# Attention scores in a hybrid layer: two of three partial products stacked into one 128-row product, the third kept as 64-row pairs

## The chip, the cores and the metric

One Trainium2 chip; the kernel runs on one of its cores. The metric is the device time of one execution in microseconds (us). An engine is named as the profile names it: PE is TensorE's matmul, PEld its weight load, DVE VectorE, ACT ScalarE, POOL GpSimd, SP the engine that issues most DMAs.

## What is computed

A decoder layer over 2048 positions with width 1024: one input projection, an attention branch of 16 heads of 64 (causal, three dilations, a window of 128 steps, linear position bias), a state-space branch, an output projection of both and a layer norm. The part that matters here, for one dilation:

```python
# q pre-scaled; blocks of 128 positions of one residue; kk, vv: previous and current block
scores = jnp.einsum('bnqrhe,bnkrhe->bnrhqk', qb, kk).astype(jnp.float32)
scores = jnp.where(valid[:, None, None], scores + bias, -jnp.inf)
lse = jax.nn.logsumexp(scores, axis=-1)
p = jnp.exp(scores - lse[..., None]).astype(vv.dtype)
o = jnp.einsum('bnrhqk,bnkrhe->bnqrhe', p, vv)
...
o1, l1 = dilated_window_attention(q, k, v, slopes, DILATIONS[0])   # 1
o2, l2 = dilated_window_attention(q, k, v, slopes, DILATIONS[1])   # 4
o3, l3 = dilated_window_attention(q, k, v, slopes, DILATIONS[2])   # 16
wts = jax.nn.softmax(jnp.stack([l1, l2, l3], axis=0), axis=0)
y_att = wts[0][..., None] * o1 + wts[1][..., None] * o2 + wts[2][..., None] * o3
```

## The kernel before

The products that need float32 precision are taken with a split of each operand into a high part, rounded to fp32r, and a low part, the remainder. A product of two split operands is a sum of three: high x high, high x low, low x high.

The first stage is the input projection (`proj`, lines 102 to 112): 128 output channels at a time against 4 x 512 positions, each 512-wide bank the sum of 8 x 3 products. `fin_qk` (lines 121 to 132) evicts q and k: ScalarE writes the high part, VectorE the low one, and each goes to its own array in device memory, `d_qh`, `d_ql`, `d_kh`, `d_kl`, one for each pair of heads. Between the projections runs the state-space branch (`ssd`, lines 322 to 393).

The second stage is attention over 8 pairs of heads. A pair of heads fills the 128 partitions: head 0 in rows 0 to 63, head 1 in rows 64 to 127. `load_pair` (lines 426 to 447) loads the bias tables and v on SP's queue, and the four parts of q and k on POOL's. The tiles of q and k lie in two pools, `qk[0]` and `qk[1]`, which pairs use in turn. `permute` (lines 460 to 474) rewrites both parts of q on POOL in the order that dilation 4 or 1 wants, into `qp` (four buffers).

A pair has 24 steps: three values of `d`, four of `qd`, two of `half`; a step covers two blocks of 128 queries. `d` = 0 is dilation 16, where a residue has just one block of 128 and so none before it; `d` = 1 is dilation 4 and `d` = 2 dilation 1, with a previous block for all but the first of each residue. `permute` serves `d` = 1 and `d` = 2.

`first` (line 476) says where there is no previous block; there the scores are 128 keys wide, else 256. `scores` (lines 479 to 521) takes, for a block, the three products for both heads, each with 64 rows of contraction, the two heads one after the other (line 503), then adds the bias and takes the row's minimum on VectorE (line 511), then the exponential on ScalarE (line 519). `transposes` (line 532) turns the weights on TensorE, VectorE copies them from PSUM to `PT` (line 534), and `values` (line 552) multiplies them with v, with both heads in 64 columns each; ScalarE copies the sums to `num` (lines 557 to 562).

The order on TensorE is written out by hand (lines 746 to 772): in turn `i` come the scores of step `i`, the transposes of step `i - 2` and the values of step `i - 3`. The order on the other engines is the planner's, by a simulated time. At the end of a pair `statistics` transposes row minima and sums, writes them to `d_st`, `gather` reads them back as `cm`, and `combine` (lines 588 to 629) works out the weights of the three dilations on VectorE, sends them through `d_wd` and, on POOL (line 613), multiplies the numerators `num` (four buffers, of which a pair takes three).

The third stage is the output projection (`product`, lines 693 to 716). Its weights are split by `load_w1` and `load_w2` into tiles that attention has done with, by the names in `ring`.

Of the kernel before, what the change touches and what calls it, by code (L numbers as in the profile page):

```python
# [9 lines left out]
F32 = mybir.dt.float32  # L10
F32R = mybir.dt.float32r
# [17 lines left out]
def hybrid_layer(ctx, tc, xT, xc, w52, wv, convw, convb, dtb, alog, dskp, gcol, wout,  # L29
# [14 lines left out]

    d_qh = [dtile(f"d_qh{i}", [128, S]) for i in range(8)]
    d_ql = [dtile(f"d_ql{i}", [128, S]) for i in range(8)]
    d_kh = [dtile(f"d_kh{i}", [128, S]) for i in range(8)]
# [26 lines left out]
    with ExitStack() as c1:  # L74
# [46 lines left out]
        def fin_qk(i, scale):  # L121
            def f(ps, tb):
                hi = ev.tile([128, 512], F32R, name="ev")
                lo = ev.tile([128, 512], F32, name="ev")
                nc.scalar.activation(hi, ps, AF.Copy, scale=scale)  # L125
                nc.vector.scalar_tensor_tensor(lo, ps, scale, hi.bitcast(F32), op0=OP.mult,  # L126
                                               op1=OP.subtract)
                s = slice(tb * 512, tb * 512 + 512)
                dh, dl = (d_kh, d_kl) if scale == 1.0 else (d_qh, d_ql)
                nc.sync.dma_start(dh[i][:, s], hi.bitcast(F32))  # L130
                nc.sync.dma_start(dl[i][:, s], lo)
            return f
# [281 lines left out]
    with ExitStack() as c2:  # L414
# [11 lines left out]
        def load_pair(pr):  # L426

            A = {"pr": pr, "num": [], "tab": [], "v": [], "cur": {}}
            for d in range(3):
                tb = io.tile([128, 2, (128, 256, 256)[d]], F32, name=f"tb{d}", bufs=1)  # L430
                c0 = (512, 256, 0)[d]
                nc.sync.dma_start(tb, tabs[2 * pr:2 * pr + 2, :, c0:c0 + tb.shape[2]]
                                  .rearrange("h p c -> p h c"))
                A["tab"].append(tb)
            A["q"], A["k"] = {0: []}, []
            for x, src in (("q", d_qh), ("k", d_kh), ("q", d_ql), ("k", d_kl)):
                to = A["q"][0] if x == "q" else A["k"]
                t = qk[pr % 2].tile([128, NR, NJ], F32R, name=f"{x}{'hl'[len(to)]}")
                nc.gpsimd.dma_start(f2(t), src[pr])
                to.append(t)  # L440
            for d in range(3):
                v = io.tile([128, 16, 128], F32, name="v", bufs=3)
                nc.sync.dma_start(v, d_v[d][:, :, pr * 128:pr * 128 + 128]
                                  .rearrange("b p e -> p b e"))
                A["v"].append(v)
            A["st"] = stp.tile([128, 192], F32, name="st")
            return A
# [30 lines left out]

        def scores(A, d, qd, half):

            P = io.tile([128, 2, 2, 256], F32, name="P", bufs=3)
            tab = A["tab"][d]
            sp = [psS.tile([128, 512], F32, name="S") for h in range(2)]
            for b in range(2):
# [11 lines left out]
                else:  # L496
                    kv = lambda t: t[:, :, 8 * blk + 8 - w // 16:8 * blk + 8].rearrange(
                        "p r (h j) -> p r h j", j=8)
                    ov = lambda a: a.rearrange("p (h r j) -> p r h j", r=16, j=8)
                for m, (x, y) in enumerate(((0, 0), (0, 1), (1, 0))):  # L500
                    for h in range(2):
                        hr = slice(64 * h, 64 * h + 64)
                        nc.tensor.matmul(ov(sp[h][:, 256 * b:256 * b + w]), A["q"][d][x][hr, blk],  # L503
                                         kv(A["k"][y][hr]), start=(m == 0), stop=(m == 2))
            for h in range(2):
# [126 lines left out]
        ring = {"qp": (io, 4), "v": (io, 3), "num": (cm_, 4), "wb": (cm_, 3)}  # L632
        ring.update({f"{x}{p}{i}": (qk[i], 1) for x in "qk" for p in "hl" for i in range(2)})
        W, SP, u7, free, os_ = {}, {}, [], [], []

        def big(name, dt=F32R):
            pool, n = ring[name]
            return f2(pool.tile([128, NR, NJ], dt, name=name if n > 1 else name[:2], bufs=n))

# [49 lines left out]

        UT = ["v", "v", "kl1"]  # L690
        banks = [("S", psS), ("S", psS), ("S", psS), ("S", psS), ("T", psT), ("T", psT)]
# [54 lines left out]
        with tc.manual_schedule(engines={mybir.EngineType.PE}):  # L746
            for i in range(len(todo) + TA + 1):
                if i < len(todo):
# [42 lines left out]
        load_u(2, 1, row())  # L791
        load_w1(2, "kh1")
        os_ += [raw, r0]
# [89 lines left out]
```

## Time and profile before

| | us |
|---|---|
| median of 3 runs | 2262.6 (2258.39 to 2266.82) |
| profiled execution, its own time | 2261.54 |
| its span, first to last instruction | 2259.7 |
| PE busy | 2176.9 (96%) |
| PEld busy | 1815.1 (80%) |
| DVE busy | 1142.9 (51%) |
| ACT busy | 871.2 (39%) |
| POOL busy | 754.1 (33%) |
| mean granted TensorE clock | 0.966 |

A line of the order of time reads: start, length, engine, line of the kernel, operation, what is written `<-` what is read, the shape of the weights (rows of contraction * columns) and of the moving operand, and how often. Lengths of matmuls overlap, since they are pipelined; what a matmul costs in a stream is the distance between starts. Starts there count from the first instruction of any kind. A line of waits reads: who waited `<-` for whom, total us, times, the longest one.

### The profile page before, as it was taken

What the parts mean: (1) busy time and instruction counts of PE and PEld (TensorE: products, weight loads), DVE (VectorE), ACT (ScalarE), POOL (GpSimd) and SP (SyncE); (2) the same over time, 40 slices, a digit from 0 to 9 for tenths busy, and PEclk for the clock granted to TensorE, in tenths of its full rate; (3) what the DMA queues carried; (4) which work ended last, traced back from release to release, by engine and by line L of the source; (5) the groups of instructions that cost most, each with busy time, mean ns of one, the idle gap of its engine ahead of it and who ended that gap; (6) DMA issues with size and microseconds to landing.
All of it is one profiled execution on the core that took longest, in us unless ns stands there. A gap on an engine that the chain in (4) does not pass through costs nothing. (4 is left out here: it accounts for less than half of the span.)

```text
span 2259.7 us, 36859 instructions
## 1 busy us (share of the span) xinstructions
PE 2176.9 (96%) x13968; PEld 1815.1 (80%) x13968; DVE 1142.9 (51%) x2931; ACT 871.2 (39%) x2318; POOL 754.1 (33%) x511
## 2 busy tenths in 40 slices
PE   8999999999999999999999998889889989899998
PEld 8999888888888888888888787677777767688886
DVE  3000365562004455545434287767767886855553
ACT  4101122213112232323454376667666774322221
POOL 3100011010113555555555214446435763222121
PEclk9999999999999999999999798889888999999999
DMA  8544222222226455555543735756674656423220
GB/s 286 167 142 125 79 68 82 75 66 80 84 71 208 163 195 179 173 178 173 179 138 108 275 108 159 202 161 180 175 205 140 169 144 207 161 99 101 79 84 28
DMA packets 232449, 321.69 MB, mean 142 GB/s; under 512 B 27088, under 2 KB 166736, under 8 KB 224080
## 3 DMA queue, kind: packets, MB, share of 16 engines
q1 hardware_dynamic: 227664, 285.78, 41.5%
q0 software_dynamic: 4608, 33.56, 4.2%
q8 instruction: 110, 1.80, 0.3%
q14 instruction: 67, 0.55, 0.1%
HBM read 205.65 MB, written 113.64 MB: 141 GB/s over the span
## 5 line engine op out<-in xcount | busy, mean ns | idle before, releaser
L109 PE MATMUL pp<-xh,whi 128*128 128x512 f32 x1408 | 550.1, 391 | 0.0
L110 PE MATMUL pp<-xl,whi 128*128 128x512 f32 x1408 | 549.5, 390 | 0.0
L111 PE MATMUL pp<-xh,wlo 128*128 128x512 f32 x1408 | 548.7, 390 | 0.0
L519 ACT ACTIVATE P<-P,st 128x256 f32<-128x256 f32 (+1 forms) x768 | 345.2, 451 | 122.2 <-DVE st L511 122.0
L511 DVE CUSTOM_DVE_ANT_0 P<-S,tb 128x256 f32<-128x256 f32 (+1 forms) x768 | 234.7, 360 | 152.9 <-PE S L503 108.7
L111 PEld LDWEIGHTS pp<-xh,wlo 128*128 128x128 f32 x1408 | 264.4, 188 | 55.0
L109 PEld LDWEIGHTS pp<-xh,whi 128*128 128x128 f32 x1408 | 264.4, 188 | 54.8
L110 PEld LDWEIGHTS pp<-xl,whi 128*128 128x128 f32 x1408 | 264.5, 188 | 54.2
L99 POOL TENSOR_TENSOR wlo<-wraw,whi 128x1024 fp32r<-128x1024 f32 x44 | 106.0, 2409 | 490.0 <-ACT whi L98 490.0
L552 PE MATMUL N<-PT,v 128*64 128x128 f32 x2400 | 192.3, 301 | 49.1 <-DVE PT L534 24.1
L552 PEld LDWEIGHTS N<-PT,v 128*64 128x64 f32 x2400 | 140.9, 148 | 86.8 <-DVE PT L534 27.3
L534 DVE COPY PT<-T 128x512 f32<-128x512 f32 (+1 forms) x304 | 196.7, 676 | 2.8 <-PE T L532 2.7
L532 PE MATMUL T<-ident,P 128*128 128x128 f32 x1200 | 189.6, 298 | 7.6 <-ACT P L519 3.7
L532 PEld LDWEIGHTS T<-ident,P 128*128 128x128 f32 x1200 | 138.2, 149 | 32.9 <-ACT P L519 5.3
L519 ACT ACTIVATION_READ_ACCUMULATOR P<-P,st 128x1 f32 x768 | 144.0, 187 | 0.0
L613 POOL TENSOR_TENSOR wb<-num,wb 128x2048 f32<-128x2048 f32 x21 | 95.3, 4550 | 144.9 <-DMA wb<-d_wd 73.4
L126 DVE SCALAR_TENSOR_TENSOR ev<-pp,ev 128x512 f32<-128x512 f32 x64 | 44.1, 688 | 195.8 <-ACT ev L125 194.8
L503 PE MATMUL S<-kh,qp 64*128 64x256 f32 (+1 forms) x1024 | 140.6, 332 | 0.0
L503 PEld LDWEIGHTS S<-kh,qp 64*128 64x128 f32 x1024 | 99.7, 212 | 25.9 <-issue 24.3
L361 DVE TENSOR_SCALAR mt<-csb,cs 128x128 f32<-128x128 f32 x256 | 72.3, 353 | 74.9 <-DMA csb<-d_cs 74.9
L152 PE MATMUL pp<-vh,xh 128*128 128x384 f32 (+1 forms) x304 | 95.0, 320 | 5.5 <-ACT xh L182 5.4
L98 ACT CAST whi<-wraw 128x1024 fp32r<-128x1024 f32 x44 | 46.0, 1046 | 137.6 <-PE pp L110 134.6
(281 smaller groups left out, 3753.1 us busy)
## 6 DMA issues: line engine op xcount, KB each, us to landing
v<-d_v SPq DMA_DIRECT2D x24, 1024.0 KB
wb<-d_wd SPq DMA_DIRECT2D x48, 512.0 KB
wraw<-w SPq DMA_DIRECT2D x44, 512.0 KB
csb<-d_cs SPq DMA_DIRECT2D x32, 512.0 KB
d_v<-vt SPq DMA_DIRECT2D x64, 192.0 KB
d_za<-ev SPq DMA_DIRECT2D x32, 256.0 KB
d_xs<-cvo SPq DMA_DIRECT2D x8, 1024.0 KB
d_zs<-ez SPq DMA_DIRECT2D x8, 1024.0 KB
```

Source lines behind the costliest of these rows:

```text
L99: nc.gpsimd.tensor_tensor(lo, raw, hi.bitcast(F32), op=OP.subtract)
L109: nc.tensor.matmul(ps, hi[:, k, :], h, start=(k == 0), stop=False)
L110: nc.tensor.matmul(ps, hi[:, k, :], l, start=False, stop=False)
L111: nc.tensor.matmul(ps, lo[:, k, :], h, start=False, stop=(k == 7))
L152: nc.tensor.matmul(ps, h, vw[k][0], start=(k == 0), stop=False)
L503: nc.tensor.matmul(ov(sp[h][:, 256 * b:256 * b + w]), A["q"][d][x][hr, blk], kv(A["k"][y][hr]), start=(m == 0), stop=(m == 2))
L511: nc.vector.tensor_tensor_reduce(P[:, h, b, 256 - w:256], sp[h][:, c0:c0 + w], tab[:, h, tab.shape[2] - w:], 1.0, 3.0e38, OP.add, OP.min, ...
L519: nc.scalar.activation(p, p, AF.Exp, bias=stat(A, 0, d, h, blk), scale=-1.0, accum_out=stat(A, 1, d, h, blk))
L532: nc.tensor.transpose(tp[:, h, b], P[:, h, b, 128 * which:128 * which + 128], ident)
L534: nc.vector.tensor_copy(pt[:, :, bl[0]:2], tp[:, :, bl[0]:2])
L552: nc.tensor.matmul(nm[64 * h:64 * h + 64, bq * 128:bq * 128 + 128], v[:, k, 64 * h:64 * h + 64], pts[which][:, h, b], start=(f or not whic ...
L613: eng.tensor_tensor(wb, nums[d], wb, op=OP.mult)
```

## The change

The q parts are stored per head and stacked: for head 0 the high part in rows 0 to 63 and the low part in rows 64 to 127, for head 1 the low part first. The high part of k is loaded twice over, so that a tile `kh[h]` holds the same 64 rows in both halves. One product of 128 rows is then high x high plus low x high. The third product, high q x low k, is taken from the same stacked tile's high half as a 64-row product, for both heads one after the other. The full products come first in a turn, then the transposes, then the 64-row ones, then the values. The stacked tiles `qs` lie in the pool `io` with two buffers, so all pairs share them; `kh0`, `kh1` and `kl` take turns as before. The names of free tiles for the output weights follow.

```diff
-    d_qh = [dtile(f"d_qh{i}", [128, S]) for i in range(8)]
-    d_ql = [dtile(f"d_ql{i}", [128, S]) for i in range(8)]
+    d_qs = [dtile(f"d_qs{i}", [2, 128, S]) for i in range(8)]
...
-                dh, dl = (d_kh, d_kl) if scale == 1.0 else (d_qh, d_ql)
-                nc.sync.dma_start(dh[i][:, s], hi.bitcast(F32))
-                nc.sync.dma_start(dl[i][:, s], lo)
+                hi = hi.bitcast(F32)
+                if scale == 1.0:
+                    nc.sync.dma_start(d_kh[i][:, s], hi)
+                    nc.sync.dma_start(d_kl[i][:, s], lo)
+                else:
+                    nc.sync.dma_start(d_qs[i][0, 0:64, s], hi[0:64])
+                    nc.sync.dma_start(d_qs[i][1, 64:128, s], hi[64:128])
+                    nc.sync.dma_start(d_qs[i].rearrange("a p t -> (a p) t")[64:192, s], lo)
...
-            A["q"], A["k"] = {0: []}, []
-            for x, src in (("q", d_qh), ("k", d_kh), ("q", d_ql), ("k", d_kl)):
-                to = A["q"][0] if x == "q" else A["k"]
-                t = qk[pr % 2].tile([128, NR, NJ], F32R, name=f"{x}{'hl'[len(to)]}")
-                nc.gpsimd.dma_start(f2(t), src[pr])
-                to.append(t)
+            A["q"] = {0: [io.tile([128, NR, NJ], F32R, name="qs", bufs=2) for h in range(2)]}
+            A["kh"] = [qk[pr % 2].tile([128, NR, NJ], F32R, name=f"kh{h}") for h in range(2)]
+            A["kl"] = qk[pr % 2].tile([128, NR, NJ], F32R, name="kl")
+            for h in range(2):
+                nc.gpsimd.dma_start(f2(A["q"][0][h]), d_qs[pr][h])
+                for i in range(2):
+                    nc.gpsimd.dma_start(f2(A["kh"][h][64 * i:64 * i + 64]), d_kh[pr][64 * h:64 * h + 64])
+            nc.gpsimd.dma_start(f2(A["kl"]), d_kl[pr])
...
-        def scores(A, d, qd, half):
-
-            P = io.tile([128, 2, 2, 256], F32, name="P", bufs=3)
-            tab = A["tab"][d]
-            sp = [psS.tile([128, 512], F32, name="S") for h in range(2)]
+        def products(A, d, qd, half, low, sp):
             for b in range(2):
...
-                for m, (x, y) in enumerate(((0, 0), (0, 1), (1, 0))):
-                    for h in range(2):
-                        hr = slice(64 * h, 64 * h + 64)
-                        nc.tensor.matmul(ov(sp[h][:, 256 * b:256 * b + w]), A["q"][d][x][hr, blk],
-                                         kv(A["k"][y][hr]), start=(m == 0), stop=(m == 2))
+                for h in range(2):
+                    hr = slice(64 * h, 64 * h + 64) if low else slice(0, 128)
+                    k = A["kl"] if low else A["kh"][h]
+                    nc.tensor.matmul(ov(sp[h][:, 256 * b:256 * b + w]), A["q"][d][h][hr, blk], kv(k[hr]),
+                                     start=not (low or b), stop=bool(low and b), skip_group_check=True)
+
+        def scores(A, d, qd, half, sp):
+            P = io.tile([128, 2, 2, 256], F32, name="P", bufs=3)
+            tab = A["tab"][d]
+            products(A, d, qd, half, True, sp)
...
-                    pts[i] = scores(pairs[pr], d, qd, half)
+                    sp = [psS.tile([128, 512], F32, name="S") for h in range(2)]
+                    products(pairs[pr], d, qd, half, False, sp)
                 if 0 <= i - TA < len(todo):
                     pr, d, qd, half = todo[i - TA]
                     pts[i - TA] = transposes(d, qd, half, pts[i - TA])
+                if i < len(todo):
+                    pr, d, qd, half = todo[i]
+                    pts[i] = scores(pairs[pr], d, qd, half, sp)
...
-        r0 = big("kl0", F32)
-        load_w2(8, r0, "qh0", "kh0")
-        load_w2(10, r0, "ql0", "num")
+        r0 = big("kl_0", F32)
+        load_w2(8, r0, "kh0_0", "kh1_0")
+        load_w2(10, r0, "qs", "num")
...
-        load_w2(14, r0, "qh1", "ql1")
+        load_w2(14, r0, "qs", "kl_1")
...
-        load_w1(2, "kh1")
+        load_w1(2, "kh0_1")
```

More of the change, by code (lines that the diff above doesn't have):

```diff
@@ L632, in hybrid_layer @@
         ring = {"qp": (io, 4), "v": (io, 3), "num": (cm_, 4), "wb": (cm_, 3)}
-        ring.update({f"{x}{p}{i}": (qk[i], 1) for x in "qk" for p in "hl" for i in range(2)})
+        ring.update({f"{x}_{i}": (qk[i], 1) for x in ("kh0", "kh1", "kl") for i in range(2)})
+        ring["qs"] = (io, 2)
         W, SP, u7, free, os_ = {}, {}, [], [], []
@@ L637, in big @@
             pool, n = ring[name]
-            return f2(pool.tile([128, NR, NJ], dt, name=name if n > 1 else name[:2], bufs=n))
+            return f2(pool.tile([128, NR, NJ], dt, name=name.split("_")[0], bufs=n))
         def prep_w(e, raw, name, eng):
@@ L688, in load_u @@
             nc.vector.reciprocal(r, r)
-        UT = ["v", "v", "kl1"]
+        UT = ["v", "v", "kh1_1"]
         banks = [("S", psS), ("S", psS), ("S", psS), ("S", psS), ("T", psT), ("T", psT)]
```

## The prediction

> **What bounds the kernel now.** I read the stretches by stage first, then the order of single instructions on TensorE, then who waited for whom. The stretches: time, busy time of PE, PEld, DVE, ACT and POOL with counts, granted clock, DMA share, GB/s.
>
> ```profile
> 0.00:1265.00 1265.00, 1258.89 (x6447) 1071.02 (x6448) 469.96 (x731) 340.20 (x497) 380.11 (x289) 1.00 0.43 139
> 1265.00:1856.00 591.00, 534.15 (x5750) 433.57 (x5748) 439.50 (x1865) 411.70 (x1632) 276.48 (x185) 0.89 0.61 171
> ```
>
> The projections hold TensorE for 1259 of 1265 us. Attention, from 1265 to 1856, is what the change is about: 591 us, TensorE busy 534, but at a granted clock of 0.89. So it loses time twice: 57 us idle, and a share of the rest at the lower clock. Next, one step of dilation 1, with 256-wide blocks, at full clock: scores S, transposes T, values V.
>
> ```profile
> 1557.71 1.09 PE L532 MATMUL T<-ident,P 128*128 128x128 f32 x8
> 1558.73 1.09 PE L552 MATMUL N<-PT,v 128*64 128x128 f32 x16
> 1559.75 0.39 PE L503 MATMUL S<-kh,qp 64*128 64x256 f32 x2
> 1559.98 0.29 PE L503 MATMUL S<-kl,qp 64*128 64x256 f32 x2
> 1560.10 0.42 PE L503 MATMUL S<-kh,qp 64*128 64x256 f32 x4
> 1560.35 0.29 PE L503 MATMUL S<-kl,qp 64*128 64x256 f32 x2
> 1560.47 0.29 PE L503 MATMUL S<-kh,qp 64*128 64x256 f32 x2
> 1560.69 1.09 PE L532 MATMUL T<-ident,P 128*128 128x128 f32 x8
> ```
>
> T 1.02, V 1.02, S 0.94 us: 2.98 a step, with no idle between. The two 64-row products of a pair (one for each head) start together, and pairs follow each other at (1560.47 - 1559.98) / 4 = 0.12 us: **twelve products take six slots**. Beside the slots a block pays at its edges: the first pair holds 0.23 instead of 0.12, and from the last pair's start to the transposes it is 0.22. A light step (dilation 16, 128-wide blocks), also at full clock:
>
> ```profile
> 1349.45 0.33 PE L503 MATMUL S<-kh,qh 64*128 64x128 f32 x2
> 1349.61 0.28 PE L503 MATMUL S<-kl,qh 64*128 64x128 f32 x2
> 1350.06 0.27 PE L503 MATMUL S<-kh,ql 64*128 64x128 f32 x2
> 1350.26 0.66 PE L532 MATMUL T<-ident,P 128*128 128x128 f32 x4
> 1350.85 0.66 PE L552 MATMUL N<-PT,v 128*64 128x128 f32 x8
> 1351.44 0.33 PE L503 MATMUL S<-kh,qh 64*128 64x128 f32 x2
> ```
>
> Here S is 0.81, T 0.59, V 0.59, the step 1.99; a pair's slot is (1350.06 - 1349.61) / 4 = 0.11, the first 0.16, the last to T 0.20. The waits (total, times, longest) say where the idle time comes from:
>
> ```profile
> PE N L552 <- DVE PT L534: 24.1, 8, 6.8
> DVE mm L592 <- DMA cm<-d_st: 22.0, 7, 7.4
> PE N L552 <- ACT num L559: 20.8, 6, 4.4
> ACT num L559 <- POOL wb L613: 16.2, 7, 5.0
> ```
>
> Once a head pair VectorE stands in `combine` for the statistics to land, and values wait for the copy behind it; and once the copy of numerators waits for the buffer that the previous pair's combination frees. The change touches neither chain.
>
> **The change part by part.**
>
> *Two products as one, 128 rows deep.* Of six slots for each block, four (two pairs) become two full products, and one pair stays: 2 + 1 = 3 slots for each 128-query block, as before. So everything hangs on what a full 128-row product of 256 columns costs. The trace has none, but the value projection has 128x128 weights against 272 columns; these are the first and last of 27 in a row, and then a product of 512 columns followed by transposes, and one followed by a 64-column shape:
>
> ```profile
> 204.72 0.29 PE L152 MATMUL pp<-vh,xh 128*128 128x272 f32 x1
> 208.00 0.29 PE L154 MATMUL pp<-vh,xl 128*128 128x272 f32 x1
> ...
> 693.71 0.39 PE L110 MATMUL pp<-xl,whi 128*128 128x512 f32 x1
> 693.94 0.39 PE L111 MATMUL pp<-xh,wlo 128*128 128x512 f32 x1
> 694.17 0.60 PE L337 MATMUL ss<-ident,xs 128*128 128x128 f32 x4
> ...
> 701.77 0.39 PE L109 MATMUL pp<-xh,whi 128*128 128x512 f32 x1
> 702.09 0.33 PE L368 MATMUL ss<-mt,xdt 128*64 128x128 f32 x2
> ```
>
> 3.28 / 26 = 0.126 us for 272 columns and 0.23 for 512; on that line 256 columns take 0.12, the very slot of a pair. For 128 columns, the four transposes at 694.17 follow at (0.60 - 0.27) / 3 = 0.11, again a pair's slot (0.27 is the length of a lone one, as in the pairs' rows). Bounds for 256 columns: 0.11 and 0.126. I take 0.12: the work in slots does not fall.
>
> [...]
>
> *The order H, T, L, V* (H the full products, L the 64-row pairs). The rows above show what an edge costs: from 512 columns to transposes with the same 128*128 shape it is 0.23 us, no more than between two products (693.71 to 693.94 is also 0.23); to the 128*64 shape it is 0.32, so 0.09 for the change of shape, and then a longer first interval. H to T keeps the shape and is free. Before there were three changes of shape (V-S, S-T, T-V), after there are three (V-H, T-L, L-V). Heavy step: H = 0.23 + 3 x 0.12 = 0.59; T loses its long first interval: three intervals there are (0.66 - 0.27) = 0.39 in the light step and 0.33 at 694.17, so 1.02 - 0.06 = 0.96; L = 0.23 + 0.22 = 0.45; together 2.00 against S + T = 1.96: +0.04. Light step: H 0.16 + 3 x 0.11 = 0.49, T 0.53, L 0.16 + 0.20 = 0.36: 1.38 against 1.40: -0.02. A head pair has 14 steps with a 256-wide block and 10 without; 8 x 14 x 0.04 - 8 x 10 x 0.02 = **+3 us**. Bounds: with the slot at 0.11, 112 x 4 x 0.01 = 4.5 less, so -1.5; at 0.126, 2.7 more, so +6.
>
> *Scores are complete later.* L ends behind T, and the next-but-one T starts earlier in its step. The path in the light step:
>
> ```profile
> 1351.33 0.69 DVE L534 COPY PT<-T 128x512 f32<-128x512 f32 x1
> 1352.27 0.19 ACT L519 ACTIVATION_READ_ACCUMULATOR P<-P,st 128x1 f32 x1
> 1352.37 0.56 ACT L557 COPY num<-N 128x512 f32<-128x512 f32 x1
> ```
>
> From the last pair (1350.06) the exponentials are done at 1352.46; their transposes start at 1350.26 + 2 x 1.99 = 1354.24: 1.8 us to spare. After, the last pair starts at 0.49 + 0.53 + 0.16 = 1.18 of its step (0.61 before) and T at 0.49 (0.81 before): 0.9 are left. The copy PT of 0.69, which now becomes ready ahead of the scores, takes about 0.3 of it, and the copy of the numerators (0.56, every second step) can take the rest. So light steps may wait by tenths. Heavy steps had more time and keep about a microsecond. Bounds: 0, and 0.1 in each of 64 light steps, +6. I take **+2**, because a light stage that runs longer shortens the wait for numerators (20.8 us above), which is counted from the end of the pair before. PT, in turn, gains the length of L before V needs it, 0.3 us in each of the eight waits, too little to count.
>
> *Loads.* Per head pair POOL issues seven DMAs for four and moves 5 MB for 4.
>
> ```profile
> 1239.61 0.75 POOL L439 DMA_DIRECT2D qh<-d_qh  x1 [0.31 <-POOL y L383]
> 1240.88 0.55 POOL L439 DMA_DIRECT2D ql<-d_ql  x1
> 1245.84 2.29 POOL L467 CAST qp<-qh 128x512 fp32r<-128x512 f32 x4 [3.40 <-DMA qh<-d_qh]
> 1251.47 2.29 POOL L467 CAST qp<-ql 128x512 fp32r<-128x512 f32 x4 [3.35 <-DMA ql<-d_ql]
> ```
>
> ```profile
> POOL qh L439 <- PE S L503: 54.1, 4, 15.4
> ```
>
> Three issues of 0.55 are 1.6 us on POOL, a queue that stood idle for 54 us in front of just these loads. `qs` has two buffers, so a pair's loads wait for the light stage before it and for the second permutation; they land some 10 us later (1240.88, the issue of `ql`, to 1251.47), and the first user, a permutation, comes with the first steps of dilation 1. Zero, with that as its cover. For head pair 0 `qs` lies in the pool that takes over the projections' memory and could come late: the most is the landing again, +11; I take 0, since the first half of the activations is done 22 us (96 products of 0.23) before the end. [...] The output weights prepared in `qs` and `kl_1` find them free once the last scores are done, about where the first product starts: 0 to +2, taken +1.
>
> Sum: 3 + 2 + 1 = **+6 us**. Against the profiled execution's 2261.5 that is 2267.5; the median of the runs lies 1.1 above it, so I say **2268**, 0.2% slower than the median. What this measurement can tell from no change is about 0.5%, 11 us.
>
> **Rivals.**
>
> *The light stages slip to the lower clock (slower).* The pace of light stages differs, by window of TensorE (length, busy, granted clock, DMA):
>
> ```profile
> 1265.40:1291.30 25.90, 21.01 (x161) 0.61 0.96 309
> 1339.10:1359.10 20.00, 18.34 (x227) 1.00 0.62 190
> 1485.90:1515.00 29.10, 22.28 (x249) 0.86 0.43 127
> ```
>
> Eight light steps took 25.9 us at 0.61 and 20.0 at 1.00. The stage at 1485.90 shows that idle time and a lower clock go together: 6.8 us idle, 0.86. If the thin slack makes TensorE pause in light stages, half the pairs going from the second to the first pace cost 4 x 5.9 = 24: 2292 with the sum. It decides once pauses recur in most light stages. [...] 0.22.
>
> *H and T count as different modes.* Then a fourth edge, 0.09 plus 0.06, in 192 steps: +29, 2296. Against it stand 693.94 to 694.17. [...] 0.05.
>
> *The DVE order moves (faster).* If the copies PT, now ready first, let `combine` meet its statistics later, the 22.0 us in which VectorE stood for `cm` go: 2245. For: they are one instruction's place in a queue. Against: program order keeps four steps between the two. 0.12.
>
> *Four products for six is a gain of a third.* If each product cost half a pair's slot, 4 x 0.06 in 112 steps and 4 x 0.055 in 80 go: -45, 2218. The 0.126 of the 272-column row speaks against it. 0.04.
>
> *No change of the above kind:* 0.57 for the forecast, with 2252 to 2276 as its own range.
>
> **The numbers.** Slower by over 0.5% (above 2274): the first two rivals and a tail of the forecast, 0.30. Faster (below 2251): the other two and a little, 0.17. Same 0.53. The range takes in the prices of the first and the third rival: 2245 to 2292.
>
> **What would show it.** Right: full products at 0.12 (0.11 for 128 columns) apart, H to T without an edge, a heavy step of about 3.0 us, light 1.98. Wrong: idle TensorE in front of T with ScalarE as releaser, a clock in 1265 to 1856 other than 0.89 by some hundredths, `cm` waits that differ by over 10 us in total, or the first scores starting well after the last projection. The wait for numerators is what I expect to give a little.

## The result and the profile after

The changed kernel takes 2340.95 us (median of 4 runs, 2337.57 to 2341.43) against 2263.48 for the kernel before (4 runs, 2258.39 to 2266.82): a ratio of 1.0341, interval 1.0319 to 1.0363. It is slower by 77 us; the profiled execution has a span of 2339.6 and a mean granted clock of 0.951.

Attention as a whole, from its first scores to its last values, in the kernel before and in the kernel after (length, busy time of PE, PEld, DVE, ACT, POOL with counts, granted clock, DMA share, GB/s):

```profile
1265.40:1879.10 613.70, 556.20 (x5951) 451.62 (x5950) 454.39 (x1901) 422.84 (x1664) 290.75 (x189) 0.89 0.61 173
```

```profile
1267.20:1955.30 688.10, 570.62 (x5178) 466.58 (x5177) 450.74 (x1901) 422.52 (x1664) 299.26 (x214) 0.85 0.61 165
```

The projections, up to 1265, are as they were, with TensorE busy for 1258 us. Attention is 74 us longer. TensorE is busy 571 us of it where it was 556, at a granted clock of 0.85 where it was 0.89, and idle 117 us where it was 58: most of the loss is idle time, and a slower clock goes with it. The steps themselves are hardly longer. TensorE in order of time, a light step, then a heavy step (256-wide blocks) and what follows, both steps at full clock:

```profile
1436.63 0.64 PE L509 MATMUL S<-kh,qs 128*128 128x128 f32 x4
...
1438.62 0.67 PE L509 MATMUL S<-kh,qs 128*128 128x128 f32 x4
...
1560.98 0.74 PE L509 MATMUL S<-kh,qp 128*128 128x256 f32 x4
1561.56 1.03 PE L544 MATMUL T<-ident,P 128*128 128x128 f32 x8
1562.53 0.51 PE L509 MATMUL S<-kl,qp 64*128 64x256 f32 x4
1562.96 1.09 PE L564 MATMUL N<-PT,v 128*64 128x128 f32 x16
1563.99 0.74 PE L509 MATMUL S<-kh,qp 128*128 128x256 f32 x4
...
1571.69 0.69 PE L564 MATMUL N<-PT,v 128*64 128x128 f32 x4 [5.66 <-ACT num L571]
```

From 1560.98 to 1563.99 the heavy step takes 3.01 us (2.98 before), the light one 1.99 (1.99 before). The last line shows where time is lost: values that stand for 5.66 us on the copy of numerators. The waits of the kernel after (total, times, longest):

```profile
DVE mm L604 <- DMA cm<-d_st: 58.7, 6, 14.5
PE N L564 <- ACT num L571: 51.9, 7, 9.7
PE N L564 <- DVE PT L546: 51.7, 6, 12.9
ACT num L571 <- POOL wb L625: 29.2, 7, 6.2
```

These are the four rows that the prediction showed of before, and each has grown: 22.0 to 58.7, 20.8 to 51.9, 24.1 to 51.7, 16.2 to 29.2. They are two links of one chain. VectorE stands for the gathered statistics `cm`, so the copy `PT` behind it is late and the values wait; and because the combination ends late, the buffer of numerators comes free late. That chain belongs to `statistics`, `gather` and `combine`, of which the change edits no line.

**What reaches that chain, for more than half of the loss, is the loads.** First their rate. The table by windows for the kernel before, in a stretch with only k loads on the way (128 partitions each), and one with the weights `wb` (64 partitions each, for which one row is read 64 times):

```profile
1344.00:1348.00 4.00, 4.00 (x59) 3.30 (x55) 2.64 (x11) 2.79 (x15) 0.00 (x0) 1.00 1.07 428
1530.00:1540.00 10.00, 7.46 (x90) 6.14 (x86) 8.75 (x32) 7.20 (x28) 4.03 (x1) 1.00 1.04 221
```

and for the kernel after, the `kh` loads into 64 partitions and the `qs` loads into 128:

```profile
1428.00:1434.00 6.00, 6.00 (x72) 5.13 (x68) 4.96 (x23) 4.28 (x18) 5.98 (x11) 1.00 1.16 233
1620.00:1622.00 2.00, 0.00 (x0) 0.00 (x0) 0.00 (x0) 0.00 (x0) 2.00 (x1) 0.88 1.07 422
```

The last two columns say it: all transfer engines fully busy in each, but 428 and 422 GB/s into 128 partitions, 221 and 233 into 64. The changed kernel loads `kh` as four halves, 2 of its 5 MB a pair, and the page's row for POOL's queue (packets, MB, share of the engines' time) of the kernel before and after:

```profile
q0 software_dynamic: 4608, 33.56, 4.2%
```

```profile
q0 software_dynamic: 6016, 41.95, 6.3%
```

25% more bytes take 4.2% of 2259.7 = 95 us of all transfer engines before and 6.3% of 2339.6 = 147 after, 55% more. The rows show the rates; what makes the half they do not show.

Second, who waits. One pair's end in the kernel after, several engines in order of time (start, length; SP lines are issues of transfers):

```profile
1509.75 2.13 POOL L447 DMA_DIRECT2D kh<-d_kh  x4
...
1520.23 0.26 ACT L584 COPY sT<-N 64x128 f32<-64x128 f32 x1
1520.52 10.26 SPq L592 DMA_DIRECT2D d_st<-sT  x4
1529.03 1.08 POOL L445 DMA_DIRECT2D qs<-d_qs  x2 [12.14 <-PE S L509]
1538.01 0.30 SPq L598 DMA_DIRECT2D cm<-d_st  x1
1540.02 0.28 DVE L604 TENSOR_TENSOR mm<-cm 32x128 f32<-32x128 f32 x1 [14.32 <-DMA cm<-d_st]
1553.82 0.54 DVE L613 TENSOR_TENSOR cm<-cm,mm 32x384 f32<-32x384 f32 x1
1566.52 4.50 POOL L625 TENSOR_TENSOR wb<-num,wb 128x2048 f32<-128x2048 f32 x1 [36.41 <-DMA wb<-d_wd]
1571.05 1.07 ACT L571 COPY num<-N 128x512 f32<-128x512 f32 x2 [2.11 <-POOL wb L625]
```

and the same places in the kernel before:

```profile
1494.78 0.59 POOL L439 DMA_DIRECT2D kh<-d_kh  x1
...
1496.94 0.26 ACT L572 COPY sT<-N 64x128 f32<-64x128 f32 x1
1497.22 7.98 SPq L580 DMA_DIRECT2D d_st<-sT  x4
1507.53 0.30 SPq L586 DMA_DIRECT2D cm<-d_st  x1
1509.53 0.28 DVE L592 TENSOR_TENSOR mm<-cm 32x128 f32<-32x128 f32 x1 [7.38 <-DMA cm<-d_st]
...
1513.38 0.59 POOL L439 DMA_DIRECT2D qh<-d_qh  x1 [12.88 <-PE S L503]
...
1535.97 4.52 POOL L613 TENSOR_TENSOR wb<-num,wb 128x2048 f32<-128x2048 f32 x1 [21.47 <-DMA wb<-d_wd]
```

In both kernels the k loads go out just ahead of the statistics. From the first store of the statistics to the load of `cm` (which waits for the stores to land, 19.4 us in all eight pairs of before) it is 10.3 us before and 17.5 after. The q loads are let go by the scores of the light stage; before, they went out at 1513.38, after `cm` had landed; after, the k loads are slower, and the q loads come at 1529.03, while the statistics are still under way. By the table by windows, in steps of 3 us, the share of the transfer engines is 1.06 or more from 1512 to 1536 in the kernel after, and the stores have landed at 1538; in the kernel before it falls to 0.14 at 1506.

A quantity that I use below: **the way**, from the end of ScalarE's copy of the second statistics to the end of POOL's first multiplication, when the next pair's numerators get their buffer. In the lines above it is 1520.49 to 1571.02 = 50.5 after, 1497.20 to 1540.49 = 43.3 before. It has three parts: landing (to the first minimum, `mm`), combination (to the end of its last product), and the rest (weights out through `d_wd`, back, first multiplication). The mean over seven pairs, worked out for each kernel from the records of these four instructions in its profiled execution:

| | landing | combination | rest | way | first statistics |
|---|---|---|---|---|---|
| before | 8.8 | 8.8 | 20.1 | 37.6 | 1348.2 |
| after | 14.8 | 14.5 | 17.7 | 47.0 | 1357.8 |

The last column is when the first pair's statistics are copied, so 9.6 us is the later start. 9.6 + 7 x 9.4 = 75 of the 77 us. The way had grown by 6.0 in the landing and 5.7 in the combination, and lost 2.4 in the rest.

### The profile page after: what moved, and what is told of

Same layout as the page of the kernel before. It is cut to its first block, busy times and chain, and to the rows that moved or that the text cites. A ratio compares the mean times of both kernels' runs of the same rounds, so it can differ in the third digit from the quotient of the medians.

```text
span 2339.6 us, 35693 instructions
## 1 busy us (share of the span) xinstructions
PE 2195.3 (94%) x13200; PEld 1834.4 (78%) x13200; DVE 1144.1 (49%) x2931; ACT 871.4 (37%) x2318; POOL 767.9 (33%) x535
## 3 DMA queue, kind: packets, MB, share of 16 engines
q0 software_dynamic: 6016, 41.95, 6.3%
## 4 chain that ended last, share of the span: by engine, by line
PE 81%; DMA 6%; issue 6%; POOL 3%; DVE 2%; SPq 1%; ACT 1%; DVEq 0%; POOLq 0%; ACTq 0%
PE pp L110 13%; PE pp L108 13%; PE pp L109 13%; PE S L509 6%; PE N L564 5%; PE T L544 4%; PE S L724 3%; PE S L726 3%; PE S L725 3%; PE pp L158 2%; PE pp L156 2%; PE pp L157 2%; DMA wb<-d_wd 2%; PE T L724 1%; PE T L725 1%
## 5 line engine op out<-in xcount | busy, mean ns | idle before, releaser
L564 PE MATMUL N<-PT,v 128*64 128x128 f32 x2400 | 195.4, 305 | 104.8 <-ACT num L571 51.9
L523 DVE CUSTOM_DVE_ANT_0 P<-S,tb 128x256 f32<-128x256 f32 (+1 forms) x768 | 233.6, 358 | 39.0 <-DMA tb<-tabs 37.6
L544 PE MATMUL T<-ident,P 128*128 128x128 f32 x1200 | 184.9, 295 | 3.8 <-DVE PT L546 2.7
L544 PEld LDWEIGHTS T<-ident,P 128*128 128x128 f32 x1200 | 147.4, 152 | 5.5 <-ACT P L531 3.2
L509 PE MATMUL S<-kh,qp 128*128 128x256 f32 (+1 forms) x512 | 107.9, 340 | 0.0
L509 PEld LDWEIGHTS S<-kh,qp 128*128 128x128 f32 x512 | 80.8, 221 | 25.7 <-issue 22.4
```

The costliest lines, as they stand in the source:

```text
L523: nc.vector.tensor_tensor_reduce(P[:, h, b, 256 - w:256], sp[h][:, c0:c0 + w], tab[:, h, tab.shape[2] - w:], 1.0, 3.0e38, OP.add, OP.min, ...
L544: nc.tensor.transpose(tp[:, h, b], P[:, h, b, 128 * which:128 * which + 128], ident)
L564: nc.tensor.matmul(nm[64 * h:64 * h + 64, bq * 128:bq * 128 + 128], v[:, k, 64 * h:64 * h + 64], pts[which][:, h, b], start=(f or not whic ...
```

## The experiments

**Is it the order of scores and transposes?** Put the order back in the changed kernel (e3), and split it in the kernel before (e4).

```diff
 # e3, from the changed kernel
                     products(pairs[pr], d, qd, half, False, sp)
+                    pts[i] = scores(pairs[pr], d, qd, half, sp)
                 if 0 <= i - TA < len(todo):
...
-                if i < len(todo):
-                    pr, d, qd, half = todo[i]
-                    pts[i] = scores(pairs[pr], d, qd, half, sp)
```

```diff
 # e4, from the kernel before: two of three pairs of products, transposes, the third pair
-                for m, (x, y) in enumerate(((0, 0), (0, 1), (1, 0))):
+                for x, y in ((0, 1),) if low else ((0, 0), (1, 0)):
...
-                    pts[i] = scores(pairs[pr], d, qd, half)
+                    sp = [psS.tile([128, 512], F32, name="S") for h in range(2)]
+                    products(pairs[pr], d, qd, half, False, sp)
...
+                if i < len(todo):
+                    pr, d, qd, half = todo[i]
+                    pts[i] = scores(pairs[pr], d, qd, half, sp)
```

> The changed kernel with the 64-row products put directly behind the full ones, ahead of the transposes, as all scores were before; loads as changed. One more change of array shape is not made: H-L, L-T, T-V, V-H are four against three. Theory O: the time falls to 2265 to 2285. Theories H and B: it stays between 2330 and 2370, the upper end from the fourth edge (0.09 to 0.15 us in 192 steps).

Measured: 2342.82 us, ratio 1.0347 (1.0323 to 1.0371), as the changed kernel. Its steps are longer by the fourth change of shape (heavy 3.14 us against 3.01, light 2.14 against 1.99, some 27 us of TensorE's time in all), so taken alone this run could hide a gain from the old order.

> The kernel before with the order of the change alone: two of the three products (as 64-row pairs still) ahead of the transposes, the third behind them; loads and tiles as before. It has two more changes of array shape in a turn (V-S, S-T, T-S, S-V against V-S, S-T, T-V: four against three). Theory O: 2320 to 2350. Theories H and B: only the added edge, about 0.15 us in 192 steps less what waits absorb, 2270 to 2295.

Measured: 2271.96 us, ratio 1.0031 (1.0006 to 1.0055). It has the order and a fourth change of shape (heavy step 3.17 us against 2.98, light 2.14 against 1.99), and both together cost 0.1 to 0.6%. So the order is not what costs 77 us.

**Is it the form of the loads?** The same bytes as before, but k in halves of 64 partitions (e2).

```diff
 # from the kernel before
-                nc.gpsimd.dma_start(f2(t), src[pr])
+                if x == "q":
+                    nc.gpsimd.dma_start(f2(t), src[pr])
+                else:
+                    for i in range(2):
+                        nc.gpsimd.dma_start(f2(t[64 * i:64 * i + 64]), src[pr][64 * i:64 * i + 64])
```

> The kernel before with one edit: the loads of the high and the low part of k are two DMAs of 64 partitions each instead of one of 128. Nothing else of the change; 4 MB for each head pair as before. Theory H: these 2 MB take about 9.5 us instead of 4.8 in front of the statistics, so some 4.7 us for each of 7 head pairs and as much again by the lower clock that follows idle time: 2295 to 2325, waits for cm of 45 to 60 us. Theories B and O: within 0.5% of 2263.

Measured: 2308.75 us, ratio 1.0214 (1.0171 to 1.0256): 45 us slower, with the old products. Its waits:

```profile
PE N L556 <- DVE PT L538: 57.2, 8, 11.7
DVE mm L596 <- DMA cm<-d_st: 55.3, 6, 12.3
```

They are what the changed kernel shows (51.7 and 58.7). So the form of the loads alone is enough to make the statistics late, with no change on TensorE. The converse, two ways to load `kh` into 128 partitions in the changed kernel: by one transfer whose source names the 64 rows twice (e1), or from a copy that is stored doubled (e5).

```diff
 # e1, from the changed kernel
-                for i in range(2):
-                    nc.gpsimd.dma_start(f2(A["kh"][h][64 * i:64 * i + 64]), d_kh[pr][64 * h:64 * h + 64])
+                nc.gpsimd.dma_start(f2(A["kh"][h]), dap(d_kh[pr], 64 * h * S, [[0, 2], [S, 64], [1, S]]))
```

> The changed kernel with one edit: each doubled tile kh[h] is filled by one DMA of 128 partitions that reads the 64 rows twice, instead of two DMAs of 64 partitions. Same bytes, same queue, same tiles. Theory H (loads into 64 partitions run at about half the rate, 0.42 to 0.5 MB in 2 us against 0.85, and stand in front of the statistics' transfers): the POOL loads go back to about 0.85 MB in 2 us, VectorE's waits for cm fall from 58.7 us towards 30, and the time to 2275 to 2295, since 1 MB more than before is still moved for each head pair. Theory B (the amount, 5 MB for 4, is what counts): no change, 2335 to 2345. Theory O (scores that are complete later, behind the transposes): no change, 2335 to 2345.

Measured: 2487.46 us, ratio 1.0993 (1.0951 to 1.1035), a miss by 192 us: this form is far worse. In the median `kh` lands 38.1 us after its issue, where the halves take 8.9, and `qs` behind it 28.8. The table by windows of e1, in a stretch in which two such loads are under way and no engine computes:

```profile
1498.00:1504.00 6.00, 0.00 (x0) 0.00 (x0) 0.00 (x0) 0.00 (x0) 0.00 (x0) 0.50 0.28 80
```

Only 0.28 of the transfer engines' time is used, 80 GB/s, and the computing engines wait. The row also holds a little of SP's transfers. Why this form leaves the transfer engines idle was not shown. The run says nothing on 64 against 128 partitions, but it is a larger dose of the same delay: `cm` is waited for 182.9 us in total and the way is 67.7 us long.

```diff
 # e5, from the changed kernel
+    d_ks = [dtile(f"d_ks{i}", [2, 128, S]) for i in range(8)]
...
-                    nc.sync.dma_start(d_kh[i][:, s], hi)
+                    for g in range(2):
+                        for r in range(2):
+                            nc.sync.dma_start(d_ks[i][g, 64 * r:64 * r + 64, s], hi[64 * g:64 * g + 64])
...
-                for i in range(2):
-                    nc.gpsimd.dma_start(f2(A["kh"][h][64 * i:64 * i + 64]), d_kh[pr][64 * h:64 * h + 64])
+                nc.gpsimd.dma_start(f2(A["kh"][h]), d_ks[pr][h])
```

> The changed kernel with the high part of k stored doubled in device memory (four half stores a tile during the projections instead of one), so that each kh[h] is filled by one plain DMA of 128 partitions. 5 MB for each head pair as changed; no load into 64 partitions is left on POOL's queue, and no source that repeats itself. Theory H (loads into 64 partitions run at half the rate and stand in front of the statistics): the loads at the stage's start take about 7 us instead of 12 to 14, the wait for cm falls from 58.7 to about 30, the time to 2275 to 2300. Theory B (5 MB for 4): 2335 to 2345.

Measured: 2296.68 us, ratio 1.0128 (1.0096 to 1.016). The same 5 MB a pair, now as transfers into 128 partitions: 44 of the 77 us are gone, and the wait for `cm` is back to what it was before the change; the wait for numerators is not. POOL's queue takes 5.0% of 2293.5 us, 115 us of all transfer engines, for the 41.95 MB that took 147 in halves: against the 95 us before, 25% more bytes now cost 21%. Waits of e5:

```profile
PE N L565 <- ACT num L572: 54.9, 7, 11.5
...
DVE mm L605 <- DMA cm<-d_st: 19.7, 5, 9.4
```

**Is it that the loads stand in the way at that moment?** Let POOL issue a pair's loads of q and k only behind the first multiplication of the combination, when the statistics have been there and back (e6, from the kernel before; e7, the same in the changed kernel; e8, the same with the doubled copy of e5).

```diff
+        held = []
         def load_pair(pr):
+            if not held:
+                return load_pair_now(pr)
+            with tc.issue_after(held[-1]):
+                return load_pair_now(pr)
+
+        def load_pair_now(pr):
...
-                eng.tensor_tensor(wb, nums[d], wb, op=OP.mult)
+                first_mul = eng.tensor_tensor(wb, nums[d], wb, op=OP.mult)
+                if d == 0 and not last:
+                    held.append(first_mul.ins)
```

> The kernel before with one edit: from head pair 2 on, the loads of q and k for the next pair stand on POOL's queue behind the first multiplication of combine, which itself waits for the statistics' whole way through device memory. So they no longer share the transfer engines with that way. Theory C (the way of the statistics, slowed by the loads in front, is what leaves TensorE idle and drops its clock): waits for cm from 22.0 to under 8, for numerators from 20.8 to under 12, clock in attention from 0.89 to 0.92 or more, time 2215 to 2245. If the loads did not matter for that way: 2255 to 2270, and more if a pair's q came late.

Measured: 2232.86 us, ratio 0.9861 (0.9845 to 0.9876), 1.4% faster than the kernel before. One pair's end in e6:

```profile
1481.94 3.74 SPq L588 DMA_DIRECT2D d_st<-sT  x4
1488.26 0.30 SPq L594 DMA_DIRECT2D cm<-d_st  x1
1490.30 0.28 DVE L600 TENSOR_TENSOR mm<-cm 32x128 f32<-32x128 f32 x1 [3.42 <-DMA cm<-d_st]
...
1509.07 4.57 POOL L621 TENSOR_TENSOR wb<-num,wb 128x2048 f32<-128x2048 f32 x1 [29.47 <-ACT P L527]
1513.58 0.60 POOL L447 DMA_DIRECT2D qh<-d_qh  x1
```

The loads now follow the multiplication, and the four stores of the statistics need 6.3 us to the load of `cm` where they needed 10.3. The way is 31.7 us against 37.6. TensorE's wait for numerators is all but gone (0.4 us); VectorE's for `cm` stays near what it was in total (19.3 us), but in shorter pieces (3.7 at most, 7.4 before), so my figure of under 8 for it was wrong. The clock in attention rises to 0.91, a little less than expected.

> The changed kernel with the loads held back in the same way, and still with the high part of k in halves of 64 partitions. Theories H and C together: the slow form costs nothing where nobody waits behind it, so nearly all of the 77 us come back and what e6 gains comes on top, less about 5 us for TensorE's longer steps: 2215 to 2260. If it were the work of TensorE or VectorE itself, 2330 to 2345.

Measured: 2291.57 us, ratio 1.0115 (1.0098 to 1.0131), 32 over the upper end. Holding takes 49 us off and leaves 7.4 us of the wait for `cm`. But by the table below the way is still 40.2 us, with 13.6 for the combination, and TensorE's wait for numerators has grown; POOL's permutation now waits for the later `qs`. Which of these costs how much the run does not show. Waits of e7:

```profile
PE N L572 <- ACT num L579: 77.4, 7, 14.8
...
POOL qp L483 <- DMA qs<-d_qs: 24.2, 5, 7.0
```

> The changed kernel with both edits, k stored doubled and the loads held back. Theories H and C: within 10 us of e7, on the lower side, 2210 to 2255. Against e6 it shows what the two stacked products are worth once the loads are out of the way: by the step lengths measured after the change (3.00 to 3.03 us against 2.97 for a heavy step) 0 to 6 us more than e6.

Measured: 2260.48 us, ratio 0.9978 (0.9966 to 0.9989): 36 us under e5, but 27.6 above e6 where I had expected 0 to 6. With the form and the moment of the loads put right, something of the change is left:

```profile
PE N L573 <- ACT num L580: 45.2, 7, 7.0
```

**What is the rest?** By the table below, e8's landing is that of e6 (7.6 and 7.7), but its combination takes 12.7 against 8.2. VectorE in e8, the chain of one combination:

```profile
1577.46 0.28 DVE L613 TENSOR_TENSOR mm<-cm 32x128 f32<-32x128 f32 x1 [2.37 <-DMA cm<-d_st]
...
1579.42 0.54 DVE L616 TENSOR_TENSOR cm<-mm,cm 32x384 f32<-32x384 f32 x1
1579.89 0.67 DVE L555 COPY PT<-T 128x512 f32<-128x512 f32 x1
...
1581.33 0.54 DVE L618 TENSOR_TENSOR cm<-cm 32x384 f32<-32x384 f32 x1
...
1587.86 0.54 DVE L622 TENSOR_TENSOR cm<-cm,mm 32x384 f32<-32x384 f32 x1
```

Between two instructions of the chain often stands a whole light step's work of VectorE, a copy `PT` and four scores with their accumulators, and then the chain advances by one instruction in 1.9 us. I first tried to put the chain ahead, with the planner's priority, in e8 (e9), e6 (e10) and the changed kernel (e11).

```diff
-                        combine(pairs.pop(pr - 1))
+                        with tc.high_priority():
+                            combine(pairs.pop(pr - 1))
```

> The kernel with doubled high parts and held loads (2260.5 us), with the ten VectorE instructions of each combination put ahead of the scores' own on VectorE. Theory (the 27 us that still part it from the kernel before with held loads, 2232.9, are a longer way through the combination: 7.5 to 11.6 us from its first minimum to its last product against 5.4 to 6.3, which the numerators' copies then wait for): ACT num<-POOL or PE N<-ACT num falls from 45 us to under 15, time 2225 to 2245. Rival (the rest is PE's own, or the 25% more bytes): the wait falls or not, the time stays at 2252 to 2265.

Measured: 2262.04 us, ratio 0.997 (0.9951 to 0.9989).

> The kernel before with held loads (2232.9 us), with the combination put first on VectorE in the same way. Theory: its numerators hardly wait (that wait is already off the list), so nothing is to be had: 2225 to 2240. Rival (the order of VectorE's instructions is worth something by itself in any kernel): 15 us or more off, under 2218.

Measured: 2233.93 us, ratio 0.986 (0.9842 to 0.9877).

> The changed kernel (2341 us), with the combination put first on VectorE and nothing else. Theory (late statistics come first, the way through the combination second; both lie in one row ahead of the numerators): num 52 us falls by 15 to 30, the gather's wait 59 us stays, time 2310 to 2335. Rival (the order on VectorE is the main cause): under 2290. Rival (not a cause): 2337 to 2345.

Measured: 2339.22 us, ratio 1.0328 (1.031 to 1.0347).

None moved. For e9 and e11 that missed what I had expected, but the combination took 12.8 us (12.7 without priority) and 14.0 (14.5): the priority did not shorten it, so the two say nothing on what a shorter one brings. Two further runs change its length by other means. In e6, five more instructions in the chain, each the maximum of a value with itself (e12):

```diff
 # from e6
             nc.vector.reciprocal(mm, mm)
+            for _ in range(5):
+                nc.vector.tensor_tensor(mm, mm, mm, op=OP.max)
```

> The kernel before with held loads (2232.9 us) and five more VectorE instructions of 32x128 in the chain of each combination, which change no value (0.28 us each, 1 to 1.5 us with what is set between them; 5 to 7 us a pair, 3 us of VectorE's own time). Theory (the last 27 us between the changed and the unchanged products, both held, are the longer way from the statistics to the first multiplication, 34 to 38 us against 28 to 34): a wait for num on PE comes up, 20 us or more, and the time goes to 2248 to 2265. Rival (that way has slack in the kernel before): 2232 to 2240, with no such wait.

Measured: 2276.53 us, ratio 1.0047 (1.0033 to 1.0061): 43.7 us more than e6, above the range of 2248 to 2265. The combination went from 8.2 to 14.8, the way from 31.7 to 39.5, and the wait came up, in e12's waits:

```profile
PE N L560 <- ACT num L567: 31.7, 7, 7.0
```

7 x 7.8 = 55 of way cost 44 of time, 0.8 for one, with the old products and the old loads. By that price e8's way, 5.2 longer than e6's, is worth 7 x 5.2 x 0.8 = 29; the difference is 27.6. So a longer way by this much is enough for it. TensorE's own time says the same: in attention it is busy 554.1 us in e8 (1266.2 to 1880.9) and 547.6 in e6 (1266.2 to 1847.1), so of the 34 us by which attention is longer in e8, 27 are idle. In e8, five of the chain's small instructions (the expectation below says six) moved to GpSimd (e13):

```diff
 # from e8; the two minima and the reciprocal stay on VectorE
+            sm = nc.vector if pr == 7 else nc.gpsimd
...
-            nc.vector.tensor_tensor(ee, mm[:, None, :].to_broadcast([32, 3, 128]), m_, op=OP.subtract)
+            sm.tensor_tensor(ee, mm[:, None, :].to_broadcast([32, 3, 128]), m_, op=OP.subtract)
...
```

> The kernel with doubled high parts and held loads (2260.5 us), with six of the nine small products and sums of each combination on GpSimd, which waits at that time, where no scores' instruction is set between them. Theory: the way from the gathered statistics to the last product falls from 11 us to 7 to 9, the wait for num from 45 us to 10 to 30, the time to 2235 to 2250. Rival (PE's own time or the 25% more bytes are the rest): the wait falls and the time stays at 2255 to 2265. If GpSimd is slower at these than VectorE with its gaps (no row of this case shows it), the way is not shorter and the run says nothing.

Measured: 2318.48 us, ratio 1.0235 (1.0213 to 1.0256). GpSimd did not shorten the chain: it took 22.2 us. In the midst of the chain GpSimd stands 49.4 us in six combinations for ScalarE's exponential and 27.7 us in seven for VectorE's reciprocal: each hop waits its turn on the other engine. TensorE's wait for numerators is 99.5 us there. So it is no test of a shorter chain, but a second one of a longer one: the way grew by 6.9 and the time by 58. All kernels side by side; the estimate is 2263.5 + (first statistics - 1348.2) + 7 x (way - 37.6), with nothing fitted:

| | landing | combination | rest | way | first statistics | estimate | measured |
|---|---|---|---|---|---|---|---|
| e10 | 7.6 | 8.7 | 15.0 | 31.2 | 1347.6 | 2218 | 2233.9 |
| e6 | 7.7 | 8.2 | 15.8 | 31.7 | 1348.4 | 2222 | 2232.9 |
| e4 | 7.1 | 9.4 | 18.8 | 35.3 | 1353.7 | 2253 | 2272.0 |
| e8 | 7.6 | 12.7 | 16.6 | 36.9 | 1351.8 | 2262 | 2260.5 |
| e9 | 7.9 | 12.8 | 16.7 | 37.3 | 1351.8 | 2265 | 2262.0 |
| before | 8.8 | 8.8 | 20.1 | 37.6 | 1348.2 | 2263.5 | 2263.5 |
| e12 | 7.7 | 14.8 | 17.0 | 39.5 | 1349.2 | 2278 | 2276.5 |
| e7 | 9.6 | 13.6 | 17.0 | 40.2 | 1357.5 | 2291 | 2291.6 |
| e5 | 9.4 | 15.0 | 16.7 | 41.1 | 1353.0 | 2293 | 2296.7 |
| e2 | 13.7 | 9.8 | 20.0 | 43.4 | 1347.2 | 2303 | 2308.8 |
| e13 | 7.6 | 22.2 | 14.1 | 43.8 | 1350.9 | 2310 | 2318.5 |
| e3 | 10.0 | 15.5 | 19.5 | 45.0 | 1360.1 | 2327 | 2342.8 |
| e11 | 15.1 | 14.0 | 17.5 | 46.6 | 1358.8 | 2337 | 2339.2 |
| after | 14.8 | 14.5 | 17.7 | 47.0 | 1357.8 | 2339 | 2341.0 |
| e1 | 37.3 | 13.3 | 17.2 | 67.7 | 1368.9 | 2495 | 2487.5 |

Over a range of 255 us the estimate is within 19, whatever the products, the order and the loads. Of the table alone one could say that a slower stage also has a longer way, since VectorE's scores stand in it. The runs that act on the way from outside show its direction: e2 and e6 touch only the loads, e12 only the chain. Where the way is short (e4, e6, e10) the kernel is 11 to 19 us above the estimate: there other things begin to count. For e4, and for e3, which is 16 above, the longer steps of TensorE are one of them.

The longer combination does not come with the form of the loads: it is 9.8 in e2, with halves and the old products, and 15.0 in e5, with plain loads and the stacked ones. It goes with VectorE's order. Counted in the records, 27 other instructions of VectorE stand between the first minimum and the last product in at least six of the seven pairs of before, e2 and e6; in after and e8 it is 45, also in at least six of seven. Open is why VectorE's queue has the combination spread wider in all kernels with the stacked products (12.7 to 15.5, but for e13's) and not in e4 (9.4), which has the split order too. The order on VectorE is the planner's, by a simulated time, so its prices for the products are the suspect; that wasn't tried.

## Where the prediction was right and where it was wrong

*The slots and edges: right.* Four products of 256 columns and the way to the transposes take 1561.56 - 1560.98 = 0.58 (predicted 0.59), T 0.97 (0.96), L 0.43 (0.45), and the heavy step 3.01 (0.03 more than before, predicted 0.04). The light step is 1.99 (1.98). A product of 128 rows costs the slot of a pair: the second one starts at 1561.20, so three and what parts them from the transposes take 0.36 us, 0.12 each, and H to T has no edge. The rivals of a third saved and of another mode are both out. The price of a fourth edge, 0.15 us a step, is what e3 and e4 show (0.13 to 0.19). By these steps TensorE's own loss is 112 x 0.03, some 3 us of the 77, as forecast; that the forecast had the right sign is luck, for the other 74 come from terms that it put at nothing or with the opposite sign. (One price of a rival is off: 2218 for a third saved is 45 below the kernel before; below the sum of 2268, from which the other rivals were counted, it is 2223.)

*Scores later, +2: not seen.* e4 has the order with a fourth edge, which the change does not have. It is 8.5 us slower, with steps that are longer by 0.15 to 0.19, first statistics that are 5.5 later, and a way that is 2.3 shorter. A term of 2 us can't be told apart in that, and no run separates it.

*Loads, zero: wrong, and the step that failed.* It was costed as issues on POOL's queue, which indeed stood idle, and as landing against the first user of the loaded tile, which indeed had time. Not asked was what else uses the transfer engines in those microseconds. The statistics of 8 KB a store and the gather go out just then, and TensorE has a chain that hangs on them. The rows were in the prediction: it showed VectorE's 22.0 us on `cm` and the 20.8 on numerators, and said of them "The change touches neither chain". It touches both, without an edited line in either. And the price of the halves stood in the trace of before, in the 221 GB/s of `wb`; 5 MB for 4 was read as 25%, and was 55% in the time of the transfer engines. By e2 and e5, the form of the loads is 44 to 45 of the 77 us. The other 33 are mostly a later start and a combination that is 5.7 us longer in each of seven pairs.

*The start, 0 of at most 11: wrong within its bounds.* It was 9.6. That this lies under 11 is luck: the bound was for the landing of q, for which the first scores did not wait, and what came late was the bias table. The halves of `kh` go out ahead of `qs`, so the permutation has its q at 1260.6, some 9 us later than the 1251.47 of before; behind it on POOL's queue go the next pair's halves, and the bias table is issued beside them. The kernel after, in order of time:

```profile
1260.62 2.30 POOL L475 CAST qp<-qs 128x512 fp32r<-128x512 f32 x4 [15.23 <-DMA qs<-d_qs]
1262.86 2.07 POOL L447 DMA_DIRECT2D kh<-d_kh  x4
1263.06 0.94 SPq L436 DMA_DIRECT2D tb<-tabs  x2
...
1277.45 0.29 DVE L523 CUSTOM_DVE_ANT_0 P<-S,tb 128x128 f32<-128x128 f32 x1 [37.65 <-DMA tb<-tabs]
1278.01 1.32 PE L509 MATMUL S<-kh,qs 128*128 128x128 f32 x4 [8.91 <-DVE st L523]
```

The first scores start at 1267.22, under 2 us later than before. VectorE gets the table only at 1277.45, 14 us after its issue (before, its first scores with the table ran at 1266.35), and the third step's scores stand for 8.91 us behind it. With `kh` doubled (e5) the same wait is 5.45 us.

*Longer light stages shorten the wait for numerators: wrong sign.* It went from 20.8 to 51.9. What decides is not when the next pair asks for the buffer, but when the combination gives it back, and that moved by more.

*The lower clock: right in direction, not as a cause.* Of the signs named for a wrong prediction two came: a clock off by some hundredths (0.85) and `cm` waits that differ by over 10 us (by 36.7). The clock went down with the chain lengthened: from 1265 to 1856, with the loads held in the kernel before, it is 0.91 with TensorE idle for 37 us, and with the chain lengthened there (e12) 0.87 with 55 us, with the same products and transfers. Idle time alone does not fix it: the kernel before has 0.89 with 57 us, e7 0.89 with 87. The rival had the idle time in the scores, at 2292; it lies in the values, at the combination.

*A DVE order that moves:* the rival named the right queue, but the opposite effect. The order on VectorE did change, with 45 other instructions in the combination instead of 27, and the ground given against it, four steps of program order, did not prevent that.

## What to carry to other kernels

When a change adds or reshapes transfers, ask not only whether their own user can wait, but which small transfers go out in the same microseconds and what hangs on them; a chain through device memory that begins with stores of 8 KB can be the pace of a whole stage: here its way is 9.4 us longer in each of seven pairs, 66 us beside the 77 that are lost. Read the rate of a transfer form from a window in which it runs alone, and cost it in time of the transfer engines rather than in bytes: here 25% more bytes took 55% more of it. And a wait that a change makes worse may be cheap to remove from the kernel before: held behind the first multiplication, the loads there give 2232.86 us, 1.4% faster than before and 4.6% faster than the change.

## What the runs showed of the hardware

In the windows shown, transfers into 64 partitions ran at 221 and 233 GB/s with all transfer engines busy (shares of 1.04 and 1.16), those into 128 at 428 and 422 (1.07 in both). Two halves didn't make a whole: the four `kh` halves were issued together and still moved 233 GB/s. In e1, two loads whose source names its 64 rows twice, with the repeat outermost, kept to 0.28 of the engines' time and 80 GB/s, and `qs`, a plain load that is issued behind them on the queue, landed 28.8 us after its issue in the median instead of 7.1.
